# The chunked recurrence of a two-block network, emitted as a pipeline in a written order

## The chip, the cores and the metric

The kernel runs on one core of a Trainium2 chip. The metric is the device time of one execution in microseconds (us). Before the change the median of three runs is 4600.68 us (4597.25 to 4603.97).

## The reference, cut to what matters

The network has a first block of two layers and a second block of one. Each layer of the first block projects 1040 tokens (16 learned ones and 1024 given), runs an attention (MLA) and a recurrence with a matrix state beside each other, joins both, and ends in a mixture of experts. The change touches the recurrence alone, whose heart is this scan over the tokens, run once forwards and once backwards, with 8 heads of 64:

```python
def step(S, inp):
    r_t, w_t, k_t, v_t, kk_t, b_t = inp
    sa = jnp.einsum('bhvk,bhk->bhv', S, kk_t)
    S = S * w_t[:, :, None, :] - sa[..., None] * b_t[:, :, None, :] + v_t[..., None] * k_t[:, :, None, :]
    return S, jnp.einsum('bhvk,bhk->bhv', S, r_t)
...
y = y_f + y_b
...
yn = ((y - mu) * lax.rsqrt(var + RWKV_GN_EPS)).reshape(B, L, RW) * gn_g + gn_b
out = (yn + (bonus_f + bonus_b).reshape(B, L, RW)) * g
```

## The kernel before, in words

The scan is done in 17 chunks of 64 tokens, in both directions at once: the forward direction lies on partitions 0 to 63, the backward one on 64 to 127. The function `recur` runs once per layer, ahead of `mla`, the attention. All products here are in fp32, and each shows as two instructions on TensorE.

For each chunk, `r_prep` loads its inputs (`ar_p`, `bk_p`), multiplies them with each other (`aa`, L785, in two halves of 16 instructions for two PSUM tiles each), masks them into `A`, and copies their diagonal blocks of 32 into the tile `dc`. Direction 0 is masked by VectorE straight from PSUM (L789); direction 1 is copied by ScalarE (L791) and masked by GpSimd (L792). `r_load` loads the chunk's inputs for the chain and transposes one of them by TensorE (`tps`, L816, then `bkt`).

A chunk's triangular system needs inverses of 32x32 blocks. `r_inv` makes them for a whole group of up to four chunks with one block of VectorE work: a transpose to `Z` (L829), 31 steps of a product `tm` and a sum `Tn` (L838, L839), and two transposes to `TF` and `TT` (L841, L843). TensorE and ScalarE then complete the inverse to 64x64 (`X`, `Xs`, `O`: 128 instructions for `X` and 128 for `O` in a group of four), which lies in `t64`.

`r_chain` is what goes from chunk to chunk. TensorE makes `Rp` (a part of the chunk's own, L884, and a part from the old state `S`, L888) and the first part of `Yp`; ScalarE copies `Rp` to `Rs`; TensorE makes `Wp` from the inverse and `Rs` (L893); ScalarE copies it into the two `uv` tiles; TensorE makes `dS` (L899); VectorE adds the old state (`tS`, L906) and multiplies by the decay (`S`, L907; L903 in the first chunk). TensorE completes `Yp` (L909), ScalarE copies it to `ys` (L911) and issues the two DMAs of `y` (L918). These are six groups of 32 instructions on TensorE.

`r_post` normalizes 128 tokens of `y` on VectorE, ScalarE and GpSimd (Square at L939, Sqrt at L942). It is emitted for each of nine tiles as soon as both directions of its tokens are written; seven in the first layer and six in the second then stand inside the chunk loop.

Nothing of the order is fixed by hand: a scheduler with a model of costs sorts the instructions of each engine, within what the source order, the dependences and the buffers allow. Each engine takes its queue in order, so that an instruction that waits holds all behind it.

Of the kernel before, what the change touches and what calls it, by code (L numbers as in the profile page):

```python
# [10 lines left out]
F32 = mybir.dt.float32  # L11
# [5 lines left out]
ALU = mybir.AluOpType  # L17
# [155 lines left out]
class K:  # L173
# [521 lines left out]
    def recur(self, li, S):  # L695
        nc, tc, I = self.nc, self.tc, self.I
        with ExitStack() as es:

            groups = ((0, 3), (3, 7), (7, 11), (11, 15), (15, 17))
            GRP = 4  # L700
# [6 lines left out]
            R["dc"] = [ep.tile([128, 32, 32], F32, name=f"dc{i}") for i in range(2)]  # L707
# [11 lines left out]
            for t in R["dc"] + R["t64"]:  # L719
                nc.gpsimd.memset(t, 0.0)  # L720

            R["pend"] = cp.tile([128, 8, 17], F32, name="pend2")
# [8 lines left out]
            ready = {}  # L731
            for i in range(9):
                lo, hi = (0, 0) if i == 0 else (2 * i - 1, 2 * i)
                ready.setdefault(max(hi, 16 - lo), []).append(i)
            LAG = 6
            A, V = {}, {}
            inv = iter(())
            for s in range(17 + LAG):
                for g, (a, b) in enumerate(groups):
                    if s == b:  # L740
                        for _ in inv:
                            pass
                        inv = self.r_inv(R, [A[c] for c in range(a, b)], g)
                        next(inv)
                    if a <= s < b:
                        dc = R["dc"][g % 2][:, 8 * (s - a):8 * (s - a) + 8]
                c = s - LAG
                if c == -1:
                    V[0] = self.r_load(R, S, 0)
                if c >= 0:  # L750
                    h, v = A.pop(c), V.pop(c)
                    while "T" not in h:
                        next(inv, None)
                    self.r_chain(R, S, c, h, v)
                next(inv, None)
                if s < 17:
                    A[s] = {"A": self.r_prep(R, S, s, dc)}
                next(inv, None)
                if 0 <= c < 16:
                    V[c + 1] = self.r_load(R, S, c + 1)  # L760
                if c >= 0:
                    for i in ready.get(c, []):
                        self.r_post(R, i)
# [11 lines left out]
    def r_prep(self, R, S, ch, dc):  # L775

        nc, st, psa = self.nc, R["st"], R["psa"]
        ar, bk = self.r_fetch(R["ap"], ("ar_p", "bk_p"), S, ch)
        A = [st.tile([128, 8, 128], F32, name="A", bufs=16) for d in range(2)]
        for z in range(0, 8, 4):  # L780
            aa = [psa.tile([128, 4, 128], F32, name="aa", tag="a") for d in range(2)]
            for h in range(4):
                for d in range(2):
                    q = slice(64 * d, 64 * d + 64)
                    nc.tensor.matmul(aa[d][:, h], bk[q, z + h], ar[q, z + h], start=True, stop=True)  # L785
# [7 lines left out]
        for d in range(2):  # L793
            for x in (64 * d, 64 * d + 32):
                nc.scalar.activation(dc[x:x + 32], A[d][x:x + 32, :, x:x + 32], AF.Copy)
        return A

    def r_load(self, R, S, ch):
# [1659 lines left out]
```

## Time and profile before

| | |
|---|---|
| median of 3 runs | 4600.68 us |
| profiled execution: time, span | 4612.27 us, 4610.5 us |
| mean granted clock of TensorE | 0.884 |
| busy, share of the span | TensorE 84%, VectorE 60%, ScalarE 41%, GpSimd 22% |

The span is the profiled execution from its first to its last instruction; its time is 1.8 us more. Busy shares are means over stages with different limits. [...] In the profiled execution the chain over the chunks, from the first state update to the last `ys`, stands from 500.6 to 813.4 us in the first layer and from 2167.0 to 2470.0 us in the second.

### The profile page before, as it was taken

The page shows a single profiled execution, that of the slowest core. Times are in us where ns is not written, and L with a number is a line of the kernel's source. Part 1 is how long each engine was busy: PE and PEld are TensorE (multiplying, and loading weights), DVE is VectorE, ACT ScalarE, POOL GpSimd, SP SyncE. Part 2 cuts the span into 40 slices and gives each one's busy share as a digit, 9 for nine tenths or more (in the row PEclk, how much of TensorE's full clock was granted, in tenths as well). Part 3 has the DMA queues.
Part 4 walks back from the last instruction along what each step waited for, and adds up shares of the span by engine and source line. Part 5 has one row for each costly group of instructions (what it writes and reads, how often), then busy time and mean ns, then how long its engine had stood idle before and what let it go on. Part 6 is the DMA issues. An engine that isn't in the chain of part 4 may idle for free.

```text
span 4610.5 us, 68074 instructions
## 1 busy us (share of the span) xinstructions
PE 3884.9 (84%) x27035; PEld 3231.2 (70%) x27035; DVE 2761.1 (60%) x4646; ACT 1895.0 (41%) x3093; POOL 1023.5 (22%) x701
## 2 busy tenths in 40 slices
PE   7888765788889868887765889699799889999998
PEld 7687655786767656766655777576588677888787
DVE  7753654756779866626364657798734753333344
ACT  4323442554268643233433542487523532111232
POOL 1423223100233243312233001342421420000000
PEclk9787777899989978785877999799899899999999
DMA  4446444104389943535543013599731131111233
GB/s 151 102 137 174 129 120 126 45 1 142 119 280 345 314 166 81 129 127 133 147 124 101 1 57 127 194 353 339 269 104 47 24 110 60 46 51 46 86 107 96
DMA packets 386200, 611.93 MB, mean 133 GB/s; under 512 B 50467, under 2 KB 217602, under 8 KB 383810
## 3 DMA queue, kind: packets, MB, share of 16 engines
q1 hardware_dynamic: 278402, 485.38, 33.6%
q10 hardware_dynamic: 90448, 79.49, 5.7%
q0 software_dynamic: 17024, 42.62, 2.9%
q8 instruction: 215, 3.52, 0.3%
q14 instruction: 111, 0.91, 0.1%
HBM read 491.65 MB, written 123.45 MB: 133 GB/s over the span
## 4 chain that ended last, share of the span: by engine, by line
PE 59%; DVE 17%; DMA 8%; ACT 6%; issue 6%; POOL 3%; ACTq 1%; SPq 0%; DVEq 0%; POOLq 0%; another core or an unknown queue 0%
PE f_mm L2349 11%; PE ms L1084 3%; DMA xw<-in_moe_w 3%; PE a_ft L1921 3%; DVE tm L838 3%; DVE Tn L839 3%; PE pp_ps L257 2%; PE pp_ps L256 2%; PE pp_ps L258 2%; PE x_hp L256 2%; PE x_hp L257 2%; PE x_hp L258 2%; PE g_mm L256 2%; PE g_mm L257 2%; PE g_mm L258 2%
## 5 line engine op out<-in xcount | busy, mean ns | idle before, releaser
L252 DVE TENSOR_TENSOR w13l<-xw,w13h 128x1024 fp32r<-128x1024 f32 x248 | 296.3, 1219 | 56.0 <-ACT w13h L251 51.2
L251 ACT ACTIVATE w13h<-xw 128x1024 fp32r<-128x1024 f32 x256 | 268.2, 1059 | 127.0 <-PE x_hp L258 83.0
L256 PE MATMUL pp_ps<-T_hi,pw_hi 128*128 128x348 f32 x912 | 310.8, 341 | 6.4 <-ACT T_hi L1687 2.5
L257 PE MATMUL pp_ps<-T_lo,pw_hi 128*128 128x348 f32 x912 | 306.4, 336 | 1.4 <-DVE T_lo L1692 1.3
L258 PE MATMUL pp_ps<-T_hi,pw_lo 128*128 128x348 f32 x912 | 305.3, 335 | 0.0
L785 PE MATMUL aa<-ar_p,bk_p 64*128 64x128 f32 x1088 | 169.8, 384 | 76.8 <-DMA bk_p<-d_BK 35.6
L2349 PE MATMUL f_mm<-F_hi,f_wh 128*128 128x512 f32 x704 | 223.0, 398 | 1.7 <-ACT F_hi L251 1.7
L2349 PE MATMUL f_mm<-F_lo,f_wh 128*128 128x512 f32 x704 | 222.8, 398 | 0.0
L2349 PE MATMUL f_mm<-F_hi,f_wl 128*128 128x512 f32 x704 | 222.6, 397 | 0.0
L785 PEld LDWEIGHTS aa<-ar_p,bk_p 64*128 64x128 f32 x1088 | 148.8, 274 | 89.0 <-DVE A L789 37.8
L256 PE MATMUL x_hp<-w13h,x_h 128*96 128x512 f32 x512 | 208.8, 408 | 0.0
L257 PE MATMUL x_hp<-w13l,x_h 128*96 128x512 f32 x512 | 205.1, 400 | 0.0
L258 PE MATMUL x_hp<-w13h,x_l 128*96 128x512 f32 x512 | 204.1, 399 | 0.0
L256 PEld LDWEIGHTS pp_ps<-T_hi,pw_hi 128*128 128x128 f32 x912 | 180.6, 198 | 19.6 <-issue 7.8
L257 PEld LDWEIGHTS pp_ps<-T_lo,pw_hi 128*128 128x128 f32 x912 | 180.8, 198 | 5.1 <-DVE T_lo L1692 2.6
L258 PEld LDWEIGHTS pp_ps<-T_hi,pw_lo 128*128 128x128 f32 x912 | 180.4, 198 | 3.0 <-issue 3.0
L1551 POOL DMA_INDIRECT d_y<-x_o,r_idx x64 | 113.9, 1780 | 304.9 <-DVE x_al L252 290.5
L287 POOL TENSOR_TENSOR g_x<-g_x,g2g 128x1024 f32<-128x1024 f32 x6 | 14.3, 2390 | 750.5 <-ACT g_x L284 750.5
L252 DVE TENSOR_TENSOR f_wl<-F_raw,f_wh 128x1024 fp32r<-128x1024 f32 x44 | 53.7, 1222 | 203.3 <-ACT f_wh L251 203.3
L251 ACT ACTIVATE f_wh<-F_raw 128x1024 fp32r<-128x1024 f32 x44 | 46.4, 1059 | 307.1 <-PE f_mm L2349 301.4
L2349 PEld LDWEIGHTS f_mm<-F_hi,f_wh 128*128 128x128 f32 x704 | 133.3, 190 | 34.2 <-ACT F_hi L251 2.0
L2349 PEld LDWEIGHTS f_mm<-F_lo,f_wh 128*128 128x128 f32 x704 | 132.9, 189 | 32.6 <-DVE F_lo L252 0.6
(628 smaller groups left out, 11368.3 us busy)
## 6 DMA issues: line engine op xcount, KB each, us to landing
xw<-in_moe_w SPq DMA_DIRECT2D x256, 512.0 KB
xw<-in_moe_w SPq DMA_DIRECT2D x64, 1024.0 KB
wd_raw<-in_w_down SPq DMA_DIRECT2D x44, 512.0 KB
pw_raw<-in_w_in SPq DMA_DIRECT2D x36, 512.0 KB
d_AR<-AR ACTq DMA_DIRECT2D x32, 544.0 KB
d_BK<-BK ACTq DMA_DIRECT2D x32, 544.0 KB
ar<-d_AR SPq DMA_DIRECT2D x68, 256.0 KB
bk<-d_BK SPq DMA_DIRECT2D x68, 256.0 KB
```

Of the source, the lines that this page charges most:

```text
L251: nc.scalar.activation(hi, src, AF.Copy)
L252: (lo_eng or nc.vector).tensor_tensor(lo, src, hi.bitcast(F32), ALU.subtract)
L256: mm(out, wh, xh, start=first, stop=False)
L257: mm(out, wh, xl, start=False, stop=False)
L258: mm(out, wl, xh, start=False, stop=last)
L785: nc.tensor.matmul(aa[d][:, h], bk[q, z + h], ar[q, z + h], start=True, stop=True)
L838: e.tensor_tensor(t, Z[:, s + 1:, s:s + 1].to_broadcast([128, a, b]), Tn[:, s:s + 1, 0:b].to_broadcast([128, a, b]), ALU.mult)
L839: e.tensor_tensor(Tn[:, s + 1:, 0:b], Tn[:, s + 1:, 0:b], t, ALU.add)
L1084: nc.tensor.matmul(sp[:n, q, :m], l[:, qt], r[:, c:c + m], start=z == 0, stop=z == 4)
L1551: nc.gpsimd.indirect_dma_start(out=y2[:, :], out_offset=bass.IndirectOffsetOnAxis(ap=si, axis=0), in_=y, in_offset=None, bounds_check=2 * ...
L1921: nc.tensor.matmul(ps[:, j], a[:, k, c], b[:, k, 512 * j:512 * j + 512], start=st, stop=sp)
L2349: nc.tensor.matmul(p[:, j], a[:, k], b[:, k, 512 * j:512 * j + 512], start=st, stop=sp)
```

## The change

TensorE, VectorE and ScalarE take the recurrence in the order in which the source emits it (`manual_schedule`); the queues of SyncE and GpSimd are still sorted by the scheduler. `recur` writes out the order: chunk by chunk the pieces of the chain, between them the two halves of the preparation of the chunk eight ahead (before: six), and bits of the next group's inverse, cut by an estimated time (`turn`). Groups are now 4, 4, 4, 4 and 1 chunks (before: 3, 4, 4, 4, 2). Apart from order:

- The old state is added to `dS` in PSUM by TensorE (`keep`: two products with the identity); VectorE's `tS` is gone.
- Both directions are masked by VectorE from PSUM; ScalarE's copy and GpSimd's product are gone.
- The diagonal of `t64` is copied from `TT` by GpSimd, before by ScalarE.
- The DMAs of `y` are issued by SyncE, before by ScalarE. There is one `dc` and one `Tn` instead of two of each.
- All nine `r_post` are emitted behind the chunk loop, outside the fixed order.

```diff
@@ recur @@
+                for c in range(N):
+                    g = c // GRP + 1
+                    hs = [A[x] for x in range(GRP * g, min(N, GRP * g + GRP))]
+                    if c % GRP == 0:
+                        inv = self.r_inv(R, hs, g) if hs else iter(())
+                        left = turn(inv, 0.0, 0.5)
+                    P = None
+                    if c + LAG < N:
+                        P = A[c + LAG] = self.r_prep(R, c + LAG)
+                    Vn = self.r_load(R, c + 1) if c + 1 < N else None
...
+                    C["state"]()
+                    C["solve"]()
+                    if P:
+                        P["halves"][0]()
+                    left = turn(inv, left, 2.2)
+                    C["keep"]()
+                    if Vn:
+                        Cn = self.r_chain(R, c + 1, A[c + 1], Vn)
+                        Cn["own"]()
+                    C["next"]()
+                    left = turn(inv, left, 0.8)
+                    if P:
+                        P["halves"][1]()
+                    C["out"]()
+                    if P:
+                        P["diag"]()
+                    left = turn(inv, left, 99.0 if c % GRP == GRP - 1 else 5.2)
+                    if Vn:
+                        Vn["bkt"]()
...
+                    if c % GRP == GRP - 1 and hs:
+                        late = self.r_solve(R, hs, g)
+                        next(late)
...
             for i in range(9):
...
+                self.r_post(R, i)
@@ r_prep @@
             for d in range(2):
-                Ah, mask = A[d][:, z:z + 4], R["mask"][d][:, None, :].to_broadcast([128, 4, 128])
-                if d == 0:
-                    nc.vector.tensor_tensor(Ah, aa[d], mask, ALU.mult)
-                else:
-                    nc.scalar.activation(Ah, aa[d], AF.Copy)
-                    nc.gpsimd.tensor_tensor(Ah, Ah, mask, ALU.mult)
...
+                nc.vector.tensor_tensor(A[d][:, z:z + 4], aa[d], R["mask"][d][:, None, :].to_broadcast([128, 4, 128]), ALU.mult)
@@ r_inv, r_solve @@
+            yield 0.36 + 0.0022 * a * b
...
-                nc.scalar.activation(t64[q:q + 32, :8 * n, 32 * hf:32 * hf + 32], TT_[q:q + 32, :8 * n], AF.Copy)
...
+                nc.gpsimd.tensor_copy(t64[q:q + 32, :8 * n, 32 * hf:32 * hf + 32], TT_[q:q + 32, :8 * n])
@@ r_chain @@
-            else:
-                ts = tp.tile([128, RW], F32, name="tS")
-                nc.vector.tensor_tensor(ts, S0, dp, ALU.add)
-                nc.vector.tensor_tensor(s1, ts.rearrange("p (h v) -> p h v", h=8), end, ALU.mult)
...
+        def keep():
+            if ch < 16:
+                dp = t["dp"] = R["psq"].tile([128, RW], F32, name="dS", tag="q")
+                if ch > 0:
+                    for d in range(2):
+                        mm(dp[own[d]], self.ident[own[d], own[d]], S0[own[d]], start=True, stop=False)
...
+        def after():
+            if ch < 16:
+                dp = t["dp"]
+                each(lambda h, d: mm(dp[own[d], x[h]], bkt[:, h, own[d]], uv[d][:, x[h]], start=ch == 0 and h == 0, stop=h == 7))
+                v = [z.rearrange("p (h v) -> p h v", h=8) for z in (S1, dp)]
+                nc.vector.tensor_tensor(v[0], v[1], R["pend"][:, :, ch:ch + 1].to_broadcast([128, 8, 64]), ALU.mult)
```

How this moves instructions shows at three places, all in the first layer. A row is a line of the source, an operation, its output and inputs, and the output's size; "x2" stands for two alike in a row.

VectorE ahead of the second and third state updates (`tS` and `S`; the number behind a name is its buffer). Before, the whole rest of the inverse stands between the first update and the second; these are its end and what follows:

```order
L838 TENSOR_TENSOR tm<-Z,Tn 128x60
L839 TENSOR_TENSOR Tn<-Tn,tm 128x2x30
L838 TENSOR_TENSOR tm<-Z,Tn 128x31
L839 TENSOR_TENSOR Tn<-Tn,tm 128x31
L841 STREAM_TRANSPOSE TF<-Tn 128x32x32
L843 STREAM_TRANSPOSE TT<-Tn 128x32x32
L789 TENSOR_TENSOR A<-aa,cmask_2842 128x512
L906 TENSOR_TENSOR tS<-S_2888,dS 128x512
L907 TENSOR_TENSOR S_2887<-tS,pend_2882 128x512
L789 TENSOR_TENSOR A<-aa,cmask_2842 128x512
L906 TENSOR_TENSOR tS<-S_2887,dS 128x512
```

After, the same engine has this around its first state updates (`S0` is written at L971):

```order
L827 TENSOR_TENSOR A_3616<-aa_3685,cmask0_2841 128x512
L827 TENSOR_TENSOR A_3617<-aa_3686,cmask1_2843 128x512
L876 TENSOR_TENSOR tm_3449<-Z_3447,Tn_3444 128x240
L877 TENSOR_TENSOR Tn_3444<-Tn_3444,tm_3449 128x20x12
L876 TENSOR_TENSOR tm_3449<-Z_3447,Tn_3444 128x247
L877 TENSOR_TENSOR Tn_3444<-Tn_3444,tm_3449 128x19x13
L971 TENSOR_TENSOR S0_2885<-dS_3701,pend2_2880 128x512
L876 TENSOR_TENSOR tm_3449<-Z_3447,Tn_3444 128x252
L877 TENSOR_TENSOR Tn_3444<-Tn_3444,tm_3449 128x18x14
```

A state update has a few steps of the inverse ahead of it instead of a run of more than twenty rows, and the masks stand between such pieces, in pairs.

ScalarE between two chunks, where the chain's copies `Rs`, `uv` and `ys` stand. Before:

```order
L891 ACTIVATE Rs<-Rp 128x512
L939 ACTIVATE q_y_6247<-q_y_6246 128x512
L895 ACTIVATE uv_6227<-Wp 64x512
L895 ACTIVATE uv_6230<-Wp 64x512
L942 ACTIVATE q_vr<-q_vr,eps_gn 128x8
L950 DMA d_yr_103<-q_y_6246 128x512
L817 ACTIVATE bkt<-tps 128x512 x2
L911 ACTIVATE ys<-Yp 128x512
```

After:

```order
L858 ACTIVATE bkt<-tps 128x512 x2
L948 ACTIVATE Rs<-Rp 128x512
L957 ACTIVATE uv_5428<-Wp 64x512
L957 ACTIVATE uv_5431<-Wp 64x512
L977 ACTIVATE ys<-Yp 128x512
L858 ACTIVATE bkt<-tps 128x512 x2
```

The chunk's copies stand by themselves; the work of `r_post` (`q_y`, `q_vr`, `d_yr`) and the DMA issues are gone from between them.

ScalarE at the first softmax of the attention (`Pm` at L1090 before and L1158 after), where it loads the table of the exponential. Before:

```order
L950 DMA d_yr_103<-q_y_6987 128x512
L1090 ACT_TABLE_LOAD
L1090 ACTIVATE Pm,s_sums<-ms,mx,s_rq 16x696
L1092 ACTIVATE Pm,s_sums<-ms,mx,s_rq 16x344
L1101 ACTIVATE Pm<-ptp 128x64
```

After:

```order
L1158 ACT_TABLE_LOAD
L1158 ACTIVATE Pm,s_sums<-ms,mx,s_rq 16x696
L1160 ACTIVATE Pm,s_sums<-ms,mx,s_rq 16x344
L1007 ACTIVATE q_y_6805<-q_y_6804 128x512
L1007 ACTIVATE q_y_6830<-q_y_6829 128x512
L1169 ACTIVATE Pm<-ptp 128x64
L1158 ACTIVATE Pm,s_sums<-ms,mx,s_rq 128x696
L1160 ACTIVATE Pm,s_sums<-ms,mx,s_rq 128x344
L1169 ACTIVATE Pm<-ptp 128x64
L1010 ACT_TABLE_LOAD
L1010 ACTIVATE q_vr<-q_vr,eps_gn 128x8 x2
L1169 ACTIVATE Pm<-ptp 16x16
```

The work of `r_post` has moved in between the softmaxes, and with its square root the table is changed to and fro: the program has 62 such loads instead of 40, 12 more in the first layer's attention and 10 more in the second's.

## Rows read from the trace of the kernel before

**Rows 1.** The chain of waits from 400 to 860 us, by line.

```profile
by line: DVE tm L838 13.3%; DVE Tn L839 12.8%; issue 9.9%; DMA d_y<-ys 3.4%; PE aa L785 3.4%; DMA q_y<-d_y 2.8%; PE dS L899 2.2%; DVE Z L829 2.1%; PE Yp L909 1.9%; DMA bk<-d_BK 1.8%; ACT t L847 1.8%; DMA bk_p<-d_BK 1.7%; DVE A L789 1.7%; AC
```

**Rows 2.** Loop, first layer: busy PE, PEld, DVE, ACT, POOL; PEclk; DMA share; GB/s.

```profile
491.70:813.40 321.70, 203.00 (x4464) 182.79 (x4464) 163.64 (x333) 120.55 (x214) 86.59 (x99) 0.78 0.45 122
```

**Rows 3.** State update lines by source: duration (minimum, median, maximum) and starts.

```profile
L903 DVE TENSOR_TENSOR S<-dS,pend x1: 682/682/682, 500.6 to 500.6; 128x512 f32<-128x512 f32 x1
...
L907 DVE TENSOR_TENSOR S<-tS,pend x15: 679/692/1745, 519.9 to 793.0; 128x512 f32<-128x512 f32 x15
...
L903 DVE TENSOR_TENSOR S<-dS,pend x1: 681/681/681, 2167.0 to 2167.0; 128x512 f32<-128x512 f32 x1
...
L907 DVE TENSOR_TENSOR S<-tS,pend x15: 641/691/1745, 2186.3 to 2461.9; 128x512 f32<-128x512 f32 x15
```

**Rows 4.** Timeline of VectorE (start, duration, row): three state updates.

```profile
546.32 0.69 DVE L907 TENSOR_TENSOR S<-tS,pend 128x512 f32<-128x512 f32 x1
...
557.51 0.69 DVE L907 TENSOR_TENSOR S<-tS,pend 128x512 f32<-128x512 f32 x1
...
580.03 0.68 DVE L907 TENSOR_TENSOR S<-tS,pend 128x512 f32<-128x512 f32 x1
```

**Rows 5.** Longest waits from 420 to 815 us.

```profile
ACT q_y L939 <- POOL q_y L938: 45.2, 7, 11.3
```

**Rows 6.** Groups by line, VectorE, from 400 to 830 us.

```profile
L838 DVE TENSOR_TENSOR tm<-Z,Tn 128x31 f32<-128x31 f32 (+15 forms) x155 | 62.3, 402 | 4.9
L839 DVE TENSOR_TENSOR Tn<-Tn,tm 128x31 f32<-128x31 f32 (+15 forms) x155 | 60.5, 390 | 4.8
L789 DVE TENSOR_TENSOR A<-aa,cmask 128x512 f32<-128x512 f32 x34 | 23.4, 687 | 82.3 <-PE aa L785 82.3
L829 DVE STREAM_TRANSPOSE Z<-dc 128x1024 f32<-128x1024 f32 x5 | 9.7, 1945 | 14.5 <-ACT dc L795 14.5
```

**Rows 7.** Timeline of TensorE while the granted clock was full.

```profile
548.84 1.09 PE L816 MATMUL tps<-ident,bk 128*128 128x128 f32 x8
...
553.08 1.15 PE L893 MATMUL Wp<-Rs,t 64*64 64x64 f32 x32 [0.49 <-ACT Rs L891]
554.15 1.16 PE L785 MATMUL aa<-ar_p,bk_p 64*128 64x128 f32 x14
555.24 0.50 PE L884 MATMUL Rp<-uv,A 128*64 128x64 f32 x9
```

**Rows 8.** Timeline of TensorE: products of 512 columns, and of the group solve.

```profile
379.08 1.02 PE L486 MATMUL g_ps<-g,gd 128*128 128x512 f32 x2
379.54 0.73 PE L258 MATMUL pp_ps<-T_hi,pw_lo 128*128 128x348 f32 x1
...
756.78 1.07 PE L857 MATMUL X<-TF,A 32*32 32x32 f32 x52
```

**Rows 9.** Half clock: a product group in the timeline, and a busy stretch.

```profile
740.90 1.97 PE L893 MATMUL Wp<-Rs,t 64*64 64x64 f32 x32
...
420.00:425.00 5.00, 5.00 (x31) 4.44 (x32) 0.24 (x2) 2.25 (x5) 1.26 (x1) 0.50 1.05 229
```

**Rows 10.** Timeline: last output copies and the first products after, either layer.

```profile
812.80 0.60 ACT L911 ACTIVATE ys<-Yp 128x512 f32<-128x512 f32 x1
...
820.05 1.23 PE L986 MATMUL ms<-cqh,wqh 128*128 128x348 f32 x3 [19.06 <-ACT wqh L251]
...
2469.39 0.60 ACT L911 ACTIVATE ys<-Yp 128x512 f32<-128x512 f32 x1 [1.23 <-PE Yp L909]
...
2486.21 1.24 PE L986 MATMUL ms<-cqh,wqh 128*128 128x348 f32 x3 [16.85 <-ACT wqh L251]
```

**Rows 11.** Attention stage of the first layer: busy time, table load.

```profile
857.70:1076.00 218.30, 196.43 (x1304) 177.92 (x1304) 133.75 (x300) 118.68 (x295) 1.17 (x4) 0.96 0.00 1
...
856.36 1.28 ACT L1090 ACT_TABLE_LOAD   x1 [5.21 <-DVE mx L1087]
857.66 0.92 ACT L1090 ACTIVATE Pm<-ms,mx,s_rq 16x696 f32<-16x696 f32 x1
```

More of the change, by code (lines that the diff above doesn't have):

```diff
@@ L909, in r_chain, with first @@
-        each(lambda h, d: mm(yp[off[d], x[h]], A[d][:, h, off[d]], uv[d][:, x[h]], start=ch == 0 and h == 0, stop=h == 7))
-        ys = tp.tile([128, RW], F32, name="ys")
-        nc.scalar.activation(ys, yp, AF.Copy)
-        for d in range(2):
-            if ch == 16 * d:
-                o = off[d].start + 48 * d
-                nc.scalar.dma_start(S["y"][d][0:NM, :], ys[o:o + NM])
-            else:
-                r0 = NM + 64 * (ch - 1) if d == 0 else T - 64 * (ch + 1)
-                nc.scalar.dma_start(S["y"][d][r0:r0 + 64, :], ys[off[d]])
+        def first():
+            rp = t["rp"] = R["psr"].tile([128, RW], F32, name="Rp", tag="r")
+            each(lambda h, d: mm(rp[own[d], x[h]], A[d][:, h, own[d]], uv[d][:, x[h]], start=h == 0, stop=ch == 0 and h == 7))
@@ new lines, in state @@
+        def state():
+            rp, yp = t["rp"], R["psq"].tile([128, RW], F32, name="Yp", tag="q")
+            t["yp"] = yp
+            if ch > 0:
+                each(lambda h, d: mm(rp[own[d], x[h]], ar[own[d], h, own[d]], S0[own[d], x[h]], start=False, stop=h == 7))
+            rs = t["rs"] = tp.tile([128, RW], F32, name="Rs")
+            nc.scalar.activation(rs, rp, AF.Copy)
+            if ch > 0:
+                each(lambda h, d: mm(yp[off[d], x[h]], ar[own[d], h, off[d]], S0[own[d], x[h]], start=h == 0, stop=False))
@@ new lines, in solve @@
+        def solve():
+            t64, s0 = H["T"]
+            wp = R["psr"].tile([128, RW], F32, name="Wp", tag="r")
+            each(lambda h, d: mm(wp[own[d], x[h]], t64[own[d], s0 + h], t["rs"][own[d], x[h]], start=True, stop=True))
+            for d in range(2):
+                nc.scalar.activation(uv[d][own[d]], wp[own[d]], AF.Copy)
+        def keep():
+            if ch < 16:
+                dp = t["dp"] = R["psq"].tile([128, RW], F32, name="dS", tag="q")
+                if ch > 0:
+                    for d in range(2):
+                        mm(dp[own[d]], self.ident[own[d], own[d]], S0[own[d]], start=True, stop=False)
@@ new lines, in after, with out @@
+        def after():
[4 more added lines that the diff above has]
+                nc.vector.tensor_tensor(v[0], v[1], R["pend"][:, :, ch:ch + 1].to_broadcast([128, 8, 64]), ALU.mult)
+        def out():
+            yp = t["yp"]
+            each(lambda h, d: mm(yp[off[d], x[h]], A[d][:, h, off[d]], uv[d][:, x[h]], start=ch == 0 and h == 0, stop=h == 7))
+            ys = tp.tile([128, RW], F32, name="ys")
+            nc.scalar.activation(ys, yp, AF.Copy)
+            for d in range(2):
+                if ch == 16 * d:
+                    o = off[d].start + 48 * d
+                    nc.sync.dma_start(S["y"][d][0:NM, :], ys[o:o + NM])
+                else:
+                    r0 = NM + 64 * (ch - 1) if d == 0 else T - 64 * (ch + 1)
+                    nc.sync.dma_start(S["y"][d][r0:r0 + 64, :], ys[off[d]])
@@ L920, in r_post @@
+        return dict(own=first, state=state, solve=solve, keep=keep, next=after, out=out)
     def r_post(self, R, i):
```

186 lines of the change are left out of this document (91 added, 95 removed).

## Prediction

> **What bounds it now.** I first read the chain of waits from 400 to 860 us, which covers the recurrence of the first layer and the start of its attention. Over a quarter of it is the two lines of the inverse on VectorE, `tm` and `Tn`, with 13.3% and 12.8% [rows 1]. An inverse is needed once in four chunks and could run beside the chain, so it should not be there. The busy times of the chunk loop say that no engine is full: of 321.7 us TensorE works 203.0 and VectorE 163.6, at a mean granted clock of 0.78 [rows 2]. So the loop is bound by the order in which work waits for work.
>
> The starts of the state updates give the size. From the first to the sixteenth, 15 periods, pass 793.0 - 500.6 = 292.4 us in the first layer and 2461.9 - 2167.0 = 294.9 in the second [rows 3], 19.5 and 19.7 for a chunk. Single periods differ: 557.51 - 546.32 = 11.2 us, then 580.03 - 557.51 = 22.5 [rows 4]. In the long ones a run of inverse rows stands in VectorE's queue ahead of the state update, as the order of before shows. ScalarE has a wait of its own: `r_post`'s square waits for GpSimd seven times in the first layer, 45.2 us in all and 11.3 at most [rows 5], while `uv` or `ys` stand behind it.
>
> **What a chunk costs in the new order.** TensorE at full clock: `Wp`, one group of 32, runs from 553.08 to the next row's start at 554.15, 1.07 us; half of `aa` from 554.15 to 555.24, 1.09; half of the transposes 1.09 [rows 7]. A product of 512 columns in two instructions takes 379.54 - 379.08 = 0.46 [rows 8]. So a chunk has six groups 6.4, `aa` 2.2, transposes 2.2, the added old state 2 x 0.46 = 0.9: 11.7 us, and 9.5 without `aa`, since the last eight chunks have no chunk eight ahead. `X` and `O` are 256 instructions for a group of four; at 1.07 for 52 [rows 8] that is 5.3 at each border of groups.
>
> VectorE: the inverse of a group is (62.3 + 60.5 + 3 x 9.7)/5 = 30.4 us, with the three transposes taken alike, 7.6 per chunk [rows 6]. Four masks at 0.69, two of them new, are 2.7 [rows 6], and the state product is 0.69; the added `tS`, about as much, is gone. Sum 11.0, and 8.3 without masks. That lies beside TensorE's 11.7 and 9.5: the new masks cost nothing while TensorE is longer, and up to 1.4 a chunk, 11 a layer, if VectorE became the bound. The written order gives a group 4 x (2.2 + 0.8 + 5.2) = 32.8 us of its own estimate for the inverse, whose steps sum by that formula to about 29; so little is left for the last bit that is emitted at once.
>
> What is not hidden is the alternation: TensorE waits for ScalarE's `Rs` (0.49 in [rows 7]) and `uv`, and for VectorE's `S`, at points where its own filler may be too short. I take 1.5 a chunk with preparation and 1.0 without, three and two times that 0.49. The lower bound is nothing; the upper is that the inverse's 2.2 + 0.8 stand ahead of `S` uncovered, 3.0 a chunk.
>
> The first eight periods hold two borders, the other seven one. 8 x (11.7 + 2 x 5.3/8 + 1.5) = 8 x 14.5 = 116.0; 7 x (9.5 + 5.3/7 + 1.0) = 7 x 11.3 = 79.1; together 195.1. Some of it will run at half clock: there the same group takes 1.97 as shown against 1.15 [rows 9, 7], a factor 1.71, so a chunk loses 0.71 x 11.7 = 8.3. I take one and a half such chunks, 12 us, with 0 and 24 as bounds: before, clock 0.78 went with TensorE busy 63% of the loop [rows 2]; the new sum has it busy about 85%. **Loop 207 us**, a gain of 85.4 in the first layer and 87.9 in the second.
>
> **What lies around the loop.**
> - Start. The preparation, the first inverse and its solve are as long as before, and two more chunks are prepared beside the inverse. I take 0, with 6 either way, about two halves of `aa` with their masks and copies.
> - Tail, from the sixteenth update to the end of the last `ys`. Before: 812.80 + 0.60 - 793.0 = 20.4 and 2469.39 + 0.60 - 2461.9 = 8.1 [rows 10, 3]. After, one chunk without preparation, 11.3: -9.1 and +3.2. The 20.4 contains an 11.3 us wait of `r_post`'s square ahead of `ys` [rows 5], which is gone.
> - From the last `ys` to the attention's first product: 6.65 and 16.2 [rows 10]. The second has more of `r_post` ahead; with none of it in the loop I take 6.65 for both: 0 and -9.6, with no change as the bound.
> - `r_post` in the attention. Seven and six tiles move there. TensorE is busy 196.4 of the 218.3 us from the first exponential on [rows 11], so there is little slack, and ScalarE stands in its chain with the softmax. The 12 and 10 added table loads, at 1.28 us [rows 11], are 15.4 and 12.8; with 5 to 7 for waits at ScalarE's head I take **20 a layer**. Lower bound: nothing, if all of it fits beside TensorE. Upper: the waits of [rows 5] come back in full, 45.
> - GpSimd's copies of `t64`'s diagonal are in no row. The nearest is VectorE's pass over a tile of this size, 1.95 [rows 6]; four are 0 to 7.8 a group, beside `X` and `O`, 5.3. I take 0, at worst 2.5 at each of three borders.
> - `y` on SyncE adds a wait there: the DMA waits for `ys`, and the loads of the next chunks stand behind it. They are about two chunks ahead in its queue, some 25 us, so 0; without that lead each chunk would wait for its loads, which would show as waits of `Rp` or `aa` for DMA.
>
> [...] By the trace the exponential starts 857.66 - 856.36 = 1.30 after its load starts [rows 11], so I see no drain behind it, and 22 loads are 28.2 us. [...]
>
> **Sum.** First layer -85.4 - 9.1 + 0 + 20 = -74.5; second -87.9 + 3.2 - 9.6 + 20 = -74.3; together -148.8. The profiled execution of 4612.3 becomes 4463.5. It lies 11.6 above the median of the runs, so the median becomes **4452 us**.
>
> **Rivals.**
> - *The attention hands back more.* `r_post`'s waits head ScalarE's queue there at 45 a layer, as [rows 5] has them. For it: the exponential needs the same engine, and TensorE is 90% busy. Against: the scheduler chooses the places, and two or three tiles stood there before. 2 x 25 = 50 more: 4502.
> - *The lock-step costs more.* The fixed order is only as good as its estimated times. If the 3.0 of inverse stands ahead of `S` in all 15 chunks, 45 instead of 19 a layer: 52 more, 4504. For it: TensorE has 0.9 of identity products and `Rp` to fill 3.0. Against: periods of 11.2 with far worse placed work.
> - *Half clock, slower than before.* TensorE stops briefly several times a chunk. At 1.71, the loop is 8 x 20.0 + 7 x 16.2 + 3 x 9.1 = 300.7, +8.3 and +5.8; tail 18.2, -2.2 and +10.1; gap -9.6; `r_post` +40: +52, 4653. For it: TensorE was busy 5.00 of 5 us at 0.50 [rows 9], so work alone did not bring the clock up at once. Against: the rows of 548 to 555 us ran at full clock with stops like the 0.49 in them [rows 7]. It decides from a loop of 207 + 74.4 = 281 on, when (281 - 195)/(301 - 195), four fifths, runs at half clock.
> - *No change*: the written order comes out like the scheduler's. Only if the loads on SyncE or the group borders set the pace at 19.5 a chunk.
>
> [...]
>
> **How the numbers follow.** The forecast has 0.62, the attention rival 0.13, the lock-step rival 0.16, no change 0.03, half clock 0.06. All but the last two are faster: 0.91; about 9 us, 0.2%, is what a measurement can tell. The bounds of the forecast's own terms reach, all good at once, 2 x (19 + 12 + 20 + 6) = 114 below, 4338, and with both rivals at once 4554. I cut the low end to 4375, since not all are good at once, and set the high end at 4560, leaving the half clock and no change out.
>
> **What would show it.** State updates 13 to 15 us apart with preparation and 11 to 12 without; no rows of `r_post` in the loop; no more than a few inverse rows between an end of `dS` and `S`; granted clock above 0.9 in the loop; 22 more table loads in the attention. It is wrong if the updates stay over 17 us apart, if the clock stays below 0.8, or if the attention grows by over 45 us a layer.

## The result and the profile after

The changed kernel takes 4420.19 us (median of 4 runs, 4414.31 to 4422.43) against 4602.33 before (4 runs): ratio 0.9604, interval 0.9587 to 0.9621. That is 182 us less; 149 were forecast. The profiled execution took 4422.43 us, 189.8 less than the one before. The two traces put the difference in these places (the attention is taken from its first product to the table load named):

| stage | before, layers 1 and 2 | after | change | forecast |
|---|---|---|---|---|
| first to sixteenth state update | 292.4, 294.8 | 186.2, 187.0 | -106.2, -107.8 | -85.4, -87.9 |
| to the end of the last `ys` | 20.4, 8.1 | 7.2, 7.2 | -13.2, -0.9 | -9.1, +3.2 |
| to the attention's first product | 6.7, 16.2 | 5.6, 5.5 | -1.0, -10.7 | 0, -9.6 |
| attention: to ScalarE's next table load (L1279, after L1347) | 280.7, 283.7 | 303.1, 312.6 | +22.3, +28.9 | +20, +20 |

The sum of these is -188.6; all else together is -1.2.

The state updates by source line; duration (minimum, median, maximum) and starts, first and second layer. They answer to [rows 3]:

```profile
L971 DVE TENSOR_TENSOR S<-dS,pend x16: 667/691/693, 500.0 to 686.2; 128x512 f32<-128x512 f32 x16
```

```profile
L971 DVE TENSOR_TENSOR S<-dS,pend x16: 652/690/692, 2070.3 to 2257.3; 128x512 f32<-128x512 f32 x16
```

VectorE's timeline: start, duration, row, and in brackets its idle time before and what ended it. Five successive updates of a stretch like that of [rows 4]:

```profile
512.66 0.69 DVE L971 TENSOR_TENSOR S<-dS,pend 128x512 f32<-128x512 f32 x1 [1.22 <-PE dS L969]
...
525.36 0.69 DVE L971 TENSOR_TENSOR S<-dS,pend 128x512 f32<-128x512 f32 x1 [1.34 <-PE dS L969]
...
538.71 0.67 DVE L971 TENSOR_TENSOR S<-dS,pend 128x512 f32<-128x512 f32 x1
...
558.53 0.69 DVE L971 TENSOR_TENSOR S<-dS,pend 128x512 f32<-128x512 f32 x1 [0.87 <-PE dS L969]
```

```profile
571.42 0.69 DVE L971 TENSOR_TENSOR S<-dS,pend 128x512 f32<-128x512 f32 x1 [1.46 <-PE dS L969]
```

The periods are 12.7, 13.4, 19.8 and 12.9 us. At four of these five updates VectorE waits for `dS` (0.87 to 1.46 us). At the third it was still at work: by its row in TensorE's timeline `dS` ended at 537.94, and the update began at 538.71. The 19.8 is the chunk that opens a group.

What TensorE waited for in the loop of the first layer (us in all, times, longest), in the kernel before and then in the changed kernel:

```profile
PE dS L899 <- ACT uv L895: 33.8, 6, 7.5
PE Rp L888 <- DVE S L907: 30.4, 6, 9.9
```

```profile
PE Wp L955 <- ACT Rs L948: 6.3, 7, 1.1
PE Rp L939 <- DMA uv<-d_v: 3.8, 5, 1.1
PE Rp L946 <- DVE S L971: 0.7, 1, 0.7
```

TensorE's waits for the state update and for ScalarE's copies `uv`, 64 us together before, are nearly gone. The second line of the changed kernel is another wait: for the DMA that loads `uv`.

Busy time, columns as in [rows 2]: the loop with its tail, and one chunk with preparation:

```profile
500.00:693.40 193.40, 170.88 (x4332) 145.31 (x4332) 133.86 (x305) 85.50 (x161) 33.91 (x54) 0.95 0.66 166
512.70:525.40 12.70, 10.85 (x238) 8.90 (x240) 10.36 (x24) 5.01 (x10) 1.04 (x2) 1.00 0.83 209
```

TensorE does 170.9 us of work in 193.4, at a granted clock of 0.95 against 0.78; within a chunk with preparation the clock is full, and TensorE is busy for 10.85 us of 12.7.

TensorE's timeline through one chunk without preparation, which answers to [rows 7]:

```profile
627.19 1.09 PE L857 MATMUL tps<-ident,bk 128*128 128x128 f32 x8
628.21 0.97 PE L946 MATMUL Rp<-S,ar 64*64 64x64 f32 x26
...
629.14 0.98 PE L950 MATMUL Yp<-S,ar 64*64 64x64 f32 x27
630.11 1.15 PE L955 MATMUL Wp<-Rs,t 64*64 64x64 f32 x32
631.10 1.03 PE L964 MATMUL dS<-S,ident 64*64 64x512 f32 x4
632.05 1.15 PE L939 MATMUL Rp<-uv,A 128*64 128x64 f32 x32
633.03 1.10 PE L969 MATMUL dS<-uv,bkt 128*64 128x64 f32 x32
633.97 1.10 PE L975 MATMUL Yp<-uv,A 128*64 128x64 f32 x32
635.00 1.09 PE L857 MATMUL tps<-ident,bk 128*128 128x128 f32 x8
```

From one transpose group's start to the next, 627.19 to 635.00, pass 7.81 us without a gap. `Rp` and `Yp` from the state take 630.11 - 628.21 = 1.90 together, `Wp` 0.99, the identity products 0.95, the transposes 628.21 - 627.19 = 1.02. So eight instructions were all the transposes of a chunk, not half: a transpose shows as one instruction (272 in the 34 chunks of both layers), where a product shows as two.

At a border of groups, first TensorE, then ScalarE:

```profile
541.21 2.34 PE L898 MATMUL X<-TF,A 32*32 32x32 f32 x128
544.92 0.95 PE L911 MATMUL O<-TT,Xs 32*32 32x32 f32 x48 [1.37 <-ACT Xs L904]
547.88 2.34 PE L911 MATMUL O<-TT,Xs 32*32 32x32 f32 x80 [2.00 <-issue]
550.15 1.65 PE L946 MATMUL Rp<-S,ar 64*64 64x64 f32 x26
```

```profile
543.68 2.41 ACT L904 ACTIVATE Xs<-X 32x512 f32<-32x512 f32 x4
548.56 1.19 ACT L913 ACTIVATE t<-O 32x512 f32<-32x512 f32 x2 [2.47 <-PE O L911]
550.26 1.19 ACT L913 ACTIVATE t<-O 32x512 f32<-32x512 f32 x2 [0.52 <-PE O L911]
```

`O` waits for the copies `Xs` (1.37) and again in its middle (2.00), and the next chunk's `Rp` starts when the copies of `O` are under way. From 541 to 552 TensorE worked 7.62 of 11 us and the granted clock was 0.76; it had been 1.00 until 538.

Last output copies and first products of the attention, as in [rows 10]:

```profile
692.82 0.60 ACT L977 ACTIVATE ys<-Yp 128x512 f32<-128x512 f32 x1 [1.28 <-issue]
```

```profile
699.06 1.23 PE L1054 MATMUL ms<-cqh,wqh 128*128 128x348 f32 x3 [6.32 <-ACT wqh L251]
```

The attention: 110 us from about the first exponential on, and the rest, columns as above; then the same 110 us in the kernel before:

```profile
739.00:849.00 110.00, 87.29 (x536) 77.97 (x535) 93.64 (x174) 71.50 (x147) 51.72 (x38) 0.91 0.22 65
849.00:1002.00 153.00, 131.89 (x891) 116.91 (x890) 91.15 (x206) 81.72 (x197) 1.40 (x5) 0.96 0.13 44
```

```profile
860.00:970.00 110.00, 102.54 (x669) 92.98 (x670) 70.55 (x156) 60.60 (x148) 0.00 (x0) 0.96 0.00 1
```

TensorE gets 15 us less done in the first 110 us, while VectorE is busy 23 us more. The stage ends with the same table load, first in the changed kernel, then in the kernel before:

```profile
1002.13 1.28 ACT L1347 ACT_TABLE_LOAD   x1
```

```profile
1100.78 1.28 ACT L1279 ACT_TABLE_LOAD   x1
```

### The profile page after: what moved, and what is told of

Same layout as the page of the kernel before. It is cut to its first block, busy times and chain, and to the rows that moved or that the text cites. A ratio compares the mean times of both kernels' runs of the same rounds, so it can differ in the third digit from the quotient of the medians.

```text
span 4420.6 us, 68400 instructions
## 1 busy us (share of the span) xinstructions
PE 3819.0 (86%) x27155; PEld 3149.8 (71%) x27155; DVE 2765.4 (63%) x4684; ACT 1846.1 (42%) x3007; POOL 971.4 (22%) x671
## 5 line engine op out<-in xcount | busy, mean ns | idle before, releaser
L825 PE MATMUL aa<-ar_p,bk_p 64*128 64x128 f32 x1088 | 131.0, 368 | 73.2 <-DMA bk_p<-d_BK 41.5
L287 POOL TENSOR_TENSOR g_x<-g_x,g2g 128x1024 f32<-128x1024 f32 x6 | 14.3, 2388 | 750.6 <-ACT g_x L284 750.6
L825 PEld LDWEIGHTS aa<-ar_p,bk_p 64*128 64x128 f32 x1088 | 110.2, 257 | 88.9 <-issue 44.3
L1619 POOL DMA_INDIRECT d_y<-x_o,r_idx x64 | 104.8, 1638 | 311.0 <-DVE x_al L252 289.4
L827 DVE TENSOR_TENSOR A<-aa,cmask 128x512 f32<-128x512 f32 x136 | 87.2, 682 | 131.2 <-PE aa L825 131.2
```

The lines of the kernel that those rows point to most:

```text
L287: e1.tensor_tensor(out[:n], out[:n], gb[:n], ALU.mult)
L825: nc.tensor.matmul(aa[d][:, h - z], bk[q, h], ar[q, h], start=True, stop=True)
L827: nc.vector.tensor_tensor(A[d][:, z:z + 4], aa[d], R["mask"][d][:, None, :].to_broadcast([128, 4, 128]), ALU.mult)
L1619: nc.gpsimd.indirect_dma_start(out=y2[:, :], out_offset=bass.IndirectOffsetOnAxis(ap=si, axis=0), in_=y, in_offset=None, bounds_check=2 * ...
```

## The experiments

Times are medians; each ratio is taken against runs of the kernel before on the same chip. These medians of the kernel before differ from chip to chip, 4600.8 to 4608.8 us, so differences of a few us between runs of the changed kernel say little. Stages are read from each run's profiled execution.

**The order left to the scheduler (free_order).**

```diff
-            with tc.manual_schedule(engines={ET.PE, ET.Activation, ET.DVE}):
+            with ExitStack():
```

> The changed kernel with the order of the recurrence left to the scheduler again; all its other edits stay (masks on VectorE, old state on TensorE, eight chunks ahead, r_post behind the loop). Theory order (the gain comes from the written order, which keeps the inverse out of the chain's way): the loop of 187 us per layer goes back to 250 to 290, the time to 4545 to 4625. Theory operations (the gain comes from the moved masks, the moved add and the relief of ScalarE and GpSimd): the loop stays below 205, the time below 4460. Theory r_post (the gain comes from its leaving the loop): the loop lies near 240, since seven waits of 45 us in all stay out of it, the time near 4530.

4488.04 us (2 runs), ratio 0.9754 (0.9735 to 0.9774): 114 of the 182 us stay. The loops take 230.0 and 210.6 us. No theory named this time: the written order is worth 68 us, and there is more than one cause. VectorE's timeline of this run, where the scheduler again put a long inverse run ahead of a state update:

```profile
542.83 0.69 DVE L971 TENSOR_TENSOR S<-dS,pend 128x512 f32<-128x512 f32 x1 [3.42 <-PE dS L969]
...
548.44 0.21 DVE L876 TENSOR_TENSOR tm<-Z,Tn 128x31 f32<-128x31 f32 x1
...
570.94 0.28 DVE L877 TENSOR_TENSOR Tn<-Tn,tm 128x112 f32<-128x112 f32 x1
571.13 0.68 DVE L971 TENSOR_TENSOR S<-dS,pend 128x512 f32<-128x512 f32 x1
```

Between the updates of 542.83 and 571.13 pass 28.3 us, with the inverse from 548.44 on ahead of the second: 56 of a group's 62 rows of `tm` and `Tn`.

**The operations of before in the written order (old_ops).** Masks, sum, the diagonal's copy and the issues of `y` as before the change:

```diff
-                nc.vector.tensor_tensor(A[d][:, z:z + 4], aa[d], R["mask"][d][:, None, :].to_broadcast([128, 4, 128]), ALU.mult)
+                Ah, mask = A[d][:, z:z + 4], R["mask"][d][:, None, :].to_broadcast([128, 4, 128])
+                if d == 0:
+                    nc.vector.tensor_tensor(Ah, aa[d], mask, ALU.mult)
+                else:
+                    nc.scalar.activation(Ah, aa[d], AF.Copy)
+                    nc.gpsimd.tensor_tensor(Ah, Ah, mask, ALU.mult)
...
-                nc.gpsimd.tensor_copy(t64[q:q + 32, :8 * n, 32 * hf:32 * hf + 32], TT_[q:q + 32, :8 * n])
+                nc.scalar.activation(t64[q:q + 32, :8 * n, 32 * hf:32 * hf + 32], TT_[q:q + 32, :8 * n], AF.Copy)
...
-                        mm(dp[own[d]], self.ident[own[d], own[d]], S0[own[d]], start=True, stop=False)
...
+                    nc.vector.tensor_tensor(ts, S0, dp, ALU.add)
...
-                    nc.sync.dma_start(S["y"][d][r0:r0 + 64, :], ys[off[d]])
+                    nc.scalar.dma_start(S["y"][d][r0:r0 + 64, :], ys[off[d]])
```

> The changed kernel in its written order, with the operations of before: direction 1 copied by ScalarE and masked by GpSimd, old state added by VectorE, diagonal of t64 copied by ScalarE, y issued by ScalarE. Theory order: the chain gets the 0.69 us sum back, 15 times, and ScalarE's four copies of 1.0 at three borders: 10 to 30 us per layer, 4440 to 4480. Theory operations: nearly all of the gain is lost, 4550 or more.

4481.66 us (2 runs), ratio 0.9740 (0.9719 to 0.9762), 61 us over the changed kernel: a little more than the theory of order allowed, far less than that of operations. The operations that I had costed at nothing matter. ScalarE's timeline at a border shows one of them:

```profile
555.49 1.19 ACT L918 ACTIVATE t<-O 32x512 f32<-32x512 f32 x2 [0.54 <-PE O L916]
556.69 4.25 ACT L922 ACTIVATE t<-TT 32x1024 f32<-32x1024 f32 x4
560.96 0.60 ACT L953 ACTIVATE Rs<-Rp 128x512 f32<-128x512 f32 x1
```

`Rs`, the chain's next step, stands behind 4.25 us of copies of the diagonal.

**The inverse in one piece (block_inverse).**

```diff
-                    left = turn(inv, left, 2.2)
+                    left = turn(inv, left, 99.0)
```

> The changed kernel with one number changed: all of a group's inverse is emitted at once in the group's first chunk, ahead of that chunk's state product on VectorE. Theory order: that chunk becomes about 25 us longer and the other three about 1 us shorter, about 22 for each of four groups, 88 per layer: 4570 to 4600. Theory operations or r_post: less than 10 per layer, below 4440.

4581.5 us (3 runs), ratio 0.9959 (0.9943 to 0.9975): 161 us of the 182 lost, as the theory of order said. The trace has it where it should be: the first update stands at 525.2 us instead of 500.0, and the loop takes 243.9 instead of 186.2. The chunk that holds the run takes 45.7 us at the first border instead of 19.8. Every other chunk is as short as in the changed kernel or shorter, 7.8 to 12.8 us. Such a run standing ahead of one state update in each group is thus enough to undo most of the change.

The loss is more than twice what the scheduler's own order costs, although there, too, 56 of the 62 rows stand together. What differs is when they start. In free_order they start at 548.44, 5.6 us behind an update, and run beside the border's `X` and `O`. Here they start at 580.56, behind masks that had to wait until TensorE was through with the border. What TensorE then waited at the first border, here and in free_order:

```profile
608.79 1.97 PE L857 MATMUL tps<-ident,bk 128*128 128x128 f32 x8 [24.27 <-DVE A L827]
```

```profile
571.87 1.14 PE L946 MATMUL Rp<-S,ar 64*64 64x64 f32 x18 [3.44 <-DVE S L971]
```

**Root on VectorE (post_newton).** The square root of `r_post` by a first guess from the bits and three Newton steps:

```diff
-        nc.scalar.activation(vr[:n], vr[:n], AF.Sqrt, scale=1.0 / 64, bias=self.eps["gn"][:n])
-        nc.vector.reciprocal(vr[:n], vr[:n])
+        x, r, w = vr[:n], tp.tile([128, 8], F32, name="q_r")[:n], tp.tile([128, 8], F32, name="q_w")[:n]
+        nc.vector.tensor_scalar(x, x, 1.0 / 64, GN_EPS, ALU.mult, ALU.add)
+        nc.vector.tensor_scalar(r.bitcast(I32), x.bitcast(I32), 1, None, ALU.logical_shift_right)
+        nc.vector.tensor_scalar(r.bitcast(I32), r.bitcast(I32), -1, 0x5F3759DF, ALU.mult, ALU.add)
+        for _ in range(3):
+            nc.vector.tensor_tensor(w, r, r, ALU.mult)
+            nc.vector.tensor_tensor(w, w, x, ALU.mult)
+            nc.vector.tensor_scalar(w, w, -0.5, 1.5, ALU.mult, ALU.add)
+            nc.vector.tensor_tensor(r, r, w, ALU.mult)
+        vr = r
```

> The changed kernel with the square root of r_post made on VectorE (a first guess from the bits and three Newton steps on 128x8 numbers) instead of ScalarE, so that no table is changed between the softmaxes. Theory tables: the 12 and 10 added loads of 1.28 us stand in the attention's chain, so 25 to 30 us come back, 4390 to 4396. Rival (the work of r_post and its waits in the queues of VectorE and ScalarE cost the attention its 22 and 29 us, the loads lie beside other waits): 0 to 8 us, 4412 to 4420.

4420.76 us (4 runs), ratio 0.9605 (0.9587 to 0.9623): no change. All loads between the softmaxes are gone, yet the attention takes 312.3 and 309.6 us. The theory of tables falls as far as this run can tell: 22 fewer loads gained nothing, but VectorE got the 15 small rows of the root per tile in exchange (the reciprocal went). Busy time of the same stretch:

```profile
739.00:849.00 110.00, 87.57 (x512) 79.62 (x513) 101.67 (x255) 50.40 (x123) 47.48 (x39) 0.85 0.22 65
```

VectorE is now busy for 101.7 of 110 us, ScalarE for 50 instead of 72, and TensorE as little as before.

**The attention without `r_post` (no_post).**

```diff
-                self.r_post(R, i)
+                c0, n = TT[i]
+                v = R["qp"].tile([128, RW], F32, name="q_v")
+                nc.sync.dma_start(v[:n], S["g"][c0:c0 + n, :])
+                nc.sync.dma_start(S["yr"][c0:c0 + n, :], v[:n])
```

> The changed kernel with the normalization of r_post left out (an input is copied to its output by two DMAs per tile), so that the attention holds none of its work. Theory VectorE (the table loads were not the cost; r_post's 38 us of VectorE work, and VectorE's rows made slower while GpSimd works, hold the attention up by 22 and 29 us): the attention falls to 278 to 285 us in both layers, the time to 4360 to 4375. Rival (the attention is longer for another reason, its lower clock after the recurrence or its later loads): it stays above 295, the time above 4395.

The whole time, 4497.85 us, lies far above the 4360 to 4375 of the theory, but says nothing here: the values behind the recurrence are others, which can send tokens to other experts, and from the attention's end to the second layer's recurrence the run took 1029.6 us against 961.8, with TensorE busy for 853.7 against 824.3. The attention itself takes 272.6 and 272.0 us, less than the 278 to 285 of the theory of VectorE. So `r_post` as a whole costs 30.5 and 40.6 there, and the rival falls; the run takes its work off every engine, so by itself it doesn't single out VectorE. Its stretch of 110 us, and two groups of VectorE in the whole attention (count, busy us, mean ns, idle before); then the same groups of the changed kernel and of the kernel before:

```profile
732.00:842.00 110.00, 100.13 (x675) 90.31 (x673) 71.36 (x158) 64.52 (x154) 0.20 (x1) 0.98 0.00 1
```

```profile
L1176 DVE TENSOR_TENSOR ptl<-Pm,pth 128x512 fp32r<-128x512 f32 (+3 forms) x108 | 51.7, 505 | 0.5
...
L1175 DVE CAST pth<-Pm 128x512 fp32r<-128x512 f32 (+3 forms) x108 | 33.8, 330 | 34.1 <-ACT Pm L1172 33.6
```

```profile
L1173 DVE TENSOR_TENSOR ptl<-Pm,pth 128x512 fp32r<-128x512 f32 (+3 forms) x108 | 56.3, 548 | 0.7
...
L1172 DVE CAST pth<-Pm 128x512 fp32r<-128x512 f32 (+3 forms) x108 | 41.1, 399 | 29.2 <-ACT Pm L1169 28.9
```

```profile
L1105 DVE TENSOR_TENSOR ptl<-Pm,pth 128x512 fp32r<-128x512 f32 (+3 forms) x108 | 51.9, 506 | 0.7
...
L1104 DVE CAST pth<-Pm 128x512 fp32r<-128x512 f32 (+3 forms) x108 | 33.7, 330 | 33.4 <-ACT Pm L1101 32.8
```

The same 108 casts `pth` take 330 ns on average where GpSimd is nearly idle and 399 where it works on `r_post`; with `ptl`, 51.7 + 33.8 us become 56.3 + 41.1. So `r_post` costs VectorE its own rows and some 12 us of slower softmax rows. That VectorE is what holds the attention up is read from these busy times; no run shows it alone.

**Single operations and moves.** The masks of direction 1 alone put back (old_masks, the first part of old_ops):

> The changed kernel with the masks of direction 1 alone put back to ScalarE's copy and GpSimd's product. The run with all operations of before lost 61 us of the gain. Theory masks (GpSimd's products slow VectorE's inverse rows while both work, and come late for the diagonal copies): 45 to 60 of it, 4465 to 4480, and tm and Tn near 0.39 and 0.41 us on average instead of 0.34. Theory chain (the 0.69 us sum on the chain and the copies on ScalarE are what cost): below 4435.

4426.6 us (2 runs), ratio 0.9609 (0.9581 to 0.9637): the masks are worth some 6 us, no more than these runs can tell. The theory of masks was right on the rows and falls on the time. Groups of VectorE from 400 to 830 us:

```profile
L881 DVE TENSOR_TENSOR tm<-Z,Tn 128x31 f32<-128x31 f32 (+15 forms) x155 | 61.7, 398 | 7.4 <-POOL Tn L873 3.2
L882 DVE TENSOR_TENSOR Tn<-Tn,tm 128x31 f32<-128x31 f32 (+15 forms) x155 | 61.3, 396 | 5.3
```

The inverse's rows are slower as forecast, near 0.40 us. In the first layer the chunks with preparation stay at 11.9 to 12.8 us all the same; only the two at borders grow, to 22.5 and 21.9 from 19.8 and 19.4.

The sum alone put back on VectorE (vector_add, the second part of old_ops):

> The changed kernel with the old state added by VectorE as before, in the written order; the identity products are gone. Masks alone cost 6 of the 61 us of the old operations. Theory chain (each state update waits 0.69 us more and TensorE has nothing else to do then): 15 times 0.69, 10 per layer, 4436 to 4445. Rival (TensorE is busy 10.9 of 12.7 us a chunk and gets back 1.0 us of identity products): 4415 to 4428, and then the remaining 45 us of the old operations lie with the copies of the diagonal and the DMA issues on ScalarE.

4421.15 us (2 runs), ratio 0.9596 (0.9577 to 0.9615): no difference in the time, and the rival holds for it. Both effects show in the trace: the chunks without preparation are longer by the sum (9.3 instead of 8.6 us, as the theory of the chain said), the one at their border is shorter (12.0 instead of 13.5), and the loops take 193.1 and 185.8 us instead of 186.2 and 187.0.

The copy of the diagonal alone put back on ScalarE (diag_scalar, the third part of old_ops):

> The changed kernel with the diagonal of t64 copied by ScalarE as before, nothing else. Of the 61 us that the old operations lost, the masks alone lost 6 and the sum on VectorE 1; this copy and the DMA issues of y on ScalarE are left. In that run the four copies, 4.25 us, stand on ScalarE ahead of Rs at each border. Theory diagonal: 3 to 4 us at three borders of a layer and at its first solve, 12 to 16 per layer, 4444 to 4454. Rival (GpSimd's copies take as long and end no earlier, so the loss lies with the issues of y between ys and the other copies, or with all of these together on a full ScalarE): 4414 to 4430.

4443.15 us (4 runs), ratio 0.9657 (0.9641 to 0.9673): 23 us lost, a hair below the range of the theory of the diagonal. The loops take 200.8 and 199.4 us, and the three chunks at borders of the first layer 23.9, 25.6 and 18.3 us instead of 19.8, 19.4 and 13.5. Of the 61 us of old_ops, 6 + 1 + 23 are found; the remaining 31 lie with the issues of `y` on ScalarE or with the four together, which was not tried.

**The kernel before with single parts of the change.** With the new operations only, order and `r_post` as before (before_new_ops; old_ops read backwards):

> The kernel before, order by the scheduler and r_post in the loop, with the new operations: both masks on VectorE, old state added by TensorE, diagonal of t64 copied by GpSimd, y issued by SyncE. If the operations give their 61 us in any order: 4535 to 4550. If they give them only in the written order, since with long inverse runs ahead of the state update VectorE is the longer engine and the masks add to it: 4585 to 4615.

4543.27 us (2 runs, 4532.72 and 4553.81), ratio 0.9862 (0.9806 to 0.9919): 63 us in the old order too, though the two runs lie far apart and the interval reaches from 37 to 89. The loops fall to 264.9 and 267.6 us.

With the nine `r_post` behind the loop only (before_posts_behind):

```diff
-                if c >= 0:
-                    for i in ready.get(c, []):
-                        self.r_post(R, i)
+            for i in range(9):
+                self.r_post(R, i)
```

> The kernel before with all nine r_post behind the loop and nothing else changed. Theory r_post: its seven waits of 45 us in all leave the loop, and its own work on VectorE and ScalarE too; the loop falls from 292 to 230 to 250 and the attention grows by 22 to 29, 4540 to 4570. Theory order: the state update still waits behind the inverse, the loop stays above 265, the time within 4580 to 4610.

4560.02 us (2 runs), ratio 0.9899 (0.9870 to 0.9927): the theory of `r_post` holds for this part. The loops take 247.7 and 251.6 us, 45 and 43 less, and the attention 315.4 and 316.3, 35 and 33 more, where 22 to 29 were expected; most of the rest is tail and gap.

**Two tries at a better version.** `r_post` spread over the attention (posts_spread; one buffer for each of its tiles instead of two, and `g` loaded later into the tile of the square):

```diff
                     if due:
                         output(*due)
...
+                    k = 4 * h + z
+                    if k in (1, 2, 4, 5, 7, 8, 10, 11, 13):
+                        self.r_post(R, next(post))
...
```

> The changed kernel with the nine r_post emitted one by one between the score groups of the attention instead of ahead of it (one buffer per tile instead of two). In the run without r_post the attention took 272.6 and 272.0 us, so its work costs 30 and 41 us there. In the changed kernel VectorE is busy 94 of the first 110 us and 91 of the last 153. Theory crowding (the work is free where VectorE has room): 15 to 25 us per layer come back, 4370 to 4392. Rival (each row of r_post on VectorE and each pass on GpSimd delays the softmax chain wherever it stands): less than 8 us for both layers, 4412 to 4428.

4416.34 us (4 runs, 4405.49 to 4432.62), ratio 0.9577 (0.9560 to 0.9595): the time is the rival's. In its profiled execution, the longest of the four, the attention takes 313.8 and 304.0 us against 303.1 and 312.6, no less in sum, with eight tiles in it instead of nine. But the edit did more than was meant: the scheduler put one tile's `r_post` into the loop, ahead of a state update. That chunk takes 19.6 and 18.6 us instead of 8.6, and the loops 196.5 and 198.6. TensorE's wait there, in the first layer:

```profile
639.60 1.65 PE L941 MATMUL Rp<-S,ar 64*64 64x64 f32 x26 [8.11 <-DVE S L966]
```

So the whole time does not test the theory cleanly; the attention alone shows no gain from spreading.

The solve of a group drawn forward (early_solve):

```diff
...
-                    left = turn(inv, left, 2.2)
+                    if c % GRP == GRP - 1 and hs:
+                        late = self.r_solve(R, hs, g)
+                        next(late)
+                    left = turn(inv, left, 3.2)
...
-                    left = turn(inv, left, 99.0 if c % GRP == GRP - 1 else 5.2)
+                    left = turn(inv, left, 99.0 if c % GRP == GRP - 2 else 6.2)
+                    for w in late:
+                        pass
...
```

> The changed kernel with the inverse done in the first three chunks of a group, X in the fourth chunk behind its Wp and O at its end, so that the next group's first chunk does not start with them. Now a chunk at a border takes 19.4 to 19.8 us against 12.7, at a clock of 0.82. Theory border (TensorE waits there for ScalarE's copies of X and O in turn): 5 to 7 us at three borders, less 1 to 2 where three chunks hold more of the inverse, 10 to 18 per layer, 4385 to 4400. Rival (VectorE becomes the longer engine with a third of the inverse per chunk, 10.1 + 3.4 = 13.5 us against 12.7): 4415 to 4430.

4417.02 us (4 runs), ratio 0.9581 (0.9564 to 0.9597), not to be told from the changed kernel. The chunk at the first border takes 14.3 us instead of 19.8, but the one before it 15.2 instead of 13.4, and the chunks without preparation up to 10.7 instead of 8.6. The loops take 184.3 and 189.7 us instead of 186.2 and 187.0. The border was real, and what it cost reappears at the chunks that hold more of the inverse: the rival.

## Why the prediction was right, and where it was not

The time lay in the range, 32 us below the forecast. By its steps:

- **Loop, 207 forecast, 186.2 and 187.0 measured.** Some 12 of the 21 us are the clock term below, 9 the chunks without preparation. The eight periods with preparation sum to 616.1 - 500.0 = 116.1 us, as forecast (116.0), but by errors that cancel: the two border chunks are 7 us longer than the others, not 5.3, and the others 11.9 to 13.4, 12.8 on average, instead of 13.2. The seven without preparation take 70.1 instead of 79.1. There the step "transposes 2.2" was mis-sized: the row was the whole of a chunk, 1.02. The lock-step of 1.0 was too much as well: in four of the seven periods TensorE has no gap, and in the others it stands still for 3.9 us together.
- **Clock, 12 a layer at half clock.** Too much: in the first layer it was full in all chunks but those at borders (0.75 to 0.83; 0.76 to 0.90 in the second), and what it cost there is within the 7 us above. The rival of half clock fell.
- **Tail and gap.** Right within some 4 us; the last chunk, taken as 11.3, took 7.2.
- **`r_post` in the attention, 20 a layer.** Size about right, 22.3 and 28.9, reason wrong. I took 15.4 and 12.8 of it for table loads. The root without loads gained nothing, and the run without `r_post` puts the whole cost on the rest of its work. The busy times point to VectorE, whose casts `pth` took 399 ns beside `r_post` against 330 without it; that part is argued.
- **"Bound by the order in which work waits for work".** Half the story. block_inverse shows the mechanism: one run of inverse rows ahead of a state update in each group loses 161 us. But the scheduler, given the other edits, loses only 68 with nearly as long a run, which starts earlier. Against the kernel before, `r_post` behind the loop is worth 46 us by itself, the new operations 63, and both with the eight-chunk lead and the new emission, in the scheduler's order, 114; the written order adds 68 for 182. What the lead and the new groups give alone was not tried.
- **Edits costed at nothing.** For masks and sum that held, as far as these runs can tell (6 and 1 us). The diagonal's copy I had at 0 to +2.5 a border; its move to GpSimd took 4 to 6 us a border off the chain, 23 in all. What failed is the step that asked only what the copies cost on the new engine: on the old one they stood ahead of `Rs`.
- **`y` on SyncE, 0.** The sign named for a missing lead, waits of `Rp` for DMA, did show, though small: five waits for the loads of `uv`, 3.8 us in the first layer's loop. In the kernel before and in old_ops, both with `y` on ScalarE, TensorE has no such wait in that loop; no run puts `y` back alone, so that SyncE is the cause is not shown.
- **VectorE in lock-step (rival).** Did not come: in a chunk with preparation VectorE is busy 10.4 of 12.7 us and mostly waits for `dS`. Where the rest of an inverse did hold an update back, TensorE had other work: it waited for `S` once in the loop, 0.7 us.

## What to carry to other kernels

When a queue holds both a chain that waits and a block of long work that is needed only later, cut the block into pieces and lay them between the chain's steps: here that was worth 161 us (block_inverse). If it must stay whole, when it starts matters: about as long a run cost far less in free_order (68 us), where it began beside other work of TensorE, than in block_inverse. Look for such blocks on every engine of the chain, since 4 us of copies ahead of a chain step on ScalarE showed in the time too (23 us). Work that is moved out of a loop comes back in part where it lands: here 46 us net of the 88 that the loops gained. Before sizing from a row, count how many instructions the source emits for the group; a row with all of them looks like one with half. And a sum that comes out right can hold errors that cancel, so set each term beside its own rows.

## What the runs showed of the hardware

- VectorE's rows were slower while GpSimd worked: the casts 399 ns against 330 above; the inverse's `tm` 402 ns [rows 6] in the kernel before, 341 in the changed kernel, where GpSimd's masks and `r_post` are gone from the loop, and 398 again with the masks alone put back (old_masks). Within one run, the changed kernel, the casts of 128x512 take 537 ns from 739 to 849 us, with GpSimd busy for 51.7 of 110 us, and 419 from 849 to 1002, with GpSimd busy for 1.4 of 153. The same groups as in [rows 6], in the changed kernel:

```profile
L877 DVE TENSOR_TENSOR Tn<-Tn,tm 128x31 f32<-128x31 f32 (+15 forms) x155 | 53.2, 343 | 5.3
L876 DVE TENSOR_TENSOR tm<-Z,Tn 128x31 f32<-128x31 f32 (+15 forms) x155 | 52.8, 341 | 7.5 <-POOL Tn L868 3.3
```

  In the run without `r_post`, with GpSimd busy for 0.20 of the 110 us shown, the casts are back at 330 ns.
- An instruction that waited held what stood behind it on its engine. In the kernel before, ScalarE's last `ys` of the first layer started at 812.80 us, though its `Yp` had ended at 801.00: ahead of it the square of `r_post` waited 11.30 us for GpSimd.
- 22 table loads of 1.28 us could be taken away for no gain (post_newton, 4420.76 us against 4420.19), when 15 small VectorE rows a tile took their place.
- TensorE kept full clock over chunk after chunk with stops of about 1 us, as here ahead of `Wp` (from 525 to 538 us TensorE was busy 11.11 of 13 us at 1.00); it was 0.76 from 541 to 552 us at the border above, with stops of 1.37 and 2.00 us. In the second layer the borders show 0.76 to 0.90.

```profile
531.59 1.15 PE L955 MATMUL Wp<-Rs,t 64*64 64x64 f32 x32 [1.09 <-ACT Rs L948]
```
